# First layer of a hybrid S5/attention block: x loaded ahead of the S5 parameters, the norm and the first products in two halves of the channels, and the copies of u's rows on GpSimd

## The chip, the core and the metric

One core of one Trainium2 chip. The metric is the device time of one execution in microseconds, median of the runs; the profile is of one further execution.

## What is computed

Two layers over 256 tokens of 1024 channels in fp32. Each has a mixer (an S5 state-space mixer in layer 0, sparse attention in layer 1) and a PEER block; a conditioning vector c gives shift, scale and gate. The change touches layer 0's mixer alone:

```
mod = silu(c) @ ada_w[0] + ada_b[0];  sh1, sc1, g1, ... = split(mod, 6)
hm  = rmsnorm(x, norm1_g[0]) * (1 + sc1) + sh1
u   = hm @ w_in
dt  = exp(log_dt);  a_bar = exp(a*dt);  b_bar = (a_bar - 1)/a * B      # complex, 64 groups of 64 states
h_t = a_bar*h_{t-1} + b_bar u_t;   y_t = Re(C h_t) + d_skip*u_t
x   = x + g1 * (ya * sigmoid(yg)),  [ya, yg] = gelu(y) @ w_glu
```

## The kernel before

x lies transposed, channels on partitions, as eight chunks of 128 x 256 (`K.xT`, KC = 8). A weight comes from HBM in units of 512 KB (`load_unit`, L129, on SyncE's queue) into a ring of six `raw` buffers. Large products run as three fp32r products (`mm3`, L188 to L190): ScalarE rounds a unit to `w_hi` (L139), VectorE takes the rest as `w_lo` (L181); the activations are split the same way into `h_hi` (L303) and `h_lo` (L304).

The modulation comes in blocks of 512 values. `ada_block` makes four units' products into a row (L201) which ScalarE copies (L204); `ada_turn` turns it into a column per 128 channels (L213) and VectorE adds the bias (L216). Of shift 1 and scale 1, blocks 0 and 2 are the first four chunks' and blocks 1 and 3 the others'.

In the norm, squares (L249, ScalarE) are summed over channels by PE (L260); `rms_scale` makes a diagonal of reciprocal roots (L273 to L277), which one product spreads over the partitions (L279). `Norm` then multiplies by norm weight and scale (`scaled`, L297) and adds the shift (`shifted`).

`s5_params` (L339 to L424) computes a_bar, its powers and the turn angles with some 45 small VectorE instructions and ScalarE functions. `Tables.first(qt)` makes angles (L471 to L479), the B table (L452 on GpSimd, L454 and L455 on VectorE, placed by ScalarE in L462) and transposes it (L496, L497); `second(qt)` makes the C table the same way and T (L508 to L524). `s5_mix` runs the eight chunks of u: `copies` writes u with four time steps beside each other into `ust`, sixteen pieces of 32 x 64 per chunk (L580, ScalarE from PSUM), and u itself (L581); `states` multiplies by the windows (L589) and scans (L594 to L609, on VectorE but for L606 on GpSimd); `outputs` adds T u and C h (L618, L623), gelu and split. `after(i)` interleaves states of chunk i - 1, outputs of chunk i - 2, one table and one modulation block with chunk i's products. Then the w_glu products.

In `s5_layer` the order of PE and ScalarE is that of the source (`manual_schedule`); VectorE, GpSimd and SyncE are ordered by a scheduler. In `s5_mix` all engines are. Each engine and queue runs in its order.

Of the kernel before, what the change touches and what calls it, by code (L numbers as in the profile page):

```python
# [8 lines left out]
F32 = mybir.dt.float32  # L9
# [183 lines left out]
def ada_block(K, layer, n):  # L193

    nc = K.nc
    ps = bank(K)
    for k2 in range(KC // 2):
        w = load_unit(K, K.aps["ada_w"][n, k2]).rearrange("p (k n) -> p k n", k=2)
        for i in range(2):
            k = 2 * k2 + i  # L200
            nc.tensor.matmul(ps[32 * (k % 4):32 * (k % 4) + 32], K.cact[:, k, :], w[:, i, :],  # L201
                             start=(k < 4), stop=(k >= 4), skip_group_check=True)
    row = K.xp.tile([P, 512], F32, name="ada_row", bufs=1)
    nc.scalar.activation(row, ps, AF.Copy)  # L204
    return lambda: ada_turn(K, layer, n, row)

# [61 lines left out]

def rms_scale(K):

    nc = K.nc
# [6 lines left out]
    rs = bank(K)[:, :S]  # L278
    nc.tensor.matmul(rs, K.ones, diag.rearrange("p t n -> p (t n)"), start=True, stop=True)  # L279
    return rs  # L280


class Norm:


    def __init__(self, K, g, layer, part, rs, bufs=4):
        self.K, self.part, self.rs, self.bufs = K, part, rs, bufs
        self.mod = K.mod[layer]
        self.sc = K.xp.tile([P, KC], F32, name="nsc")
        K.nc.vector.scalar_tensor_tensor(self.sc, self.mod[:, part + 8:part + 16], 1.0, g, op0=OP.add, op1=OP.mult)  # L290
        self.hi = K.hpool.tile([P, KC, S], F32R, name="h_hi")
        self.lo = K.hpool.tile([P, KC, S], F32R, name="h_lo")
        self.t = K.xp.tile([P, KC, S], F32, name="nt")

    def scaled(self, k):
        K = self.K
# [42 lines left out]
def s5_params(K, pp, prm):  # L339
# [11 lines left out]
    with tc.tile_pool(name="s5q", bufs=1, reuse_waits="tile") as pr:  # L351
# [73 lines left out]
class Tables:  # L425
# [37 lines left out]

    def first(self, qt):

        K, pp = self.K, self.pp
# [20 lines left out]
        self.place(lambda r, g: self.b[r, :, :, :, g], m)  # L487
        for k in range(2 * qt, 2 * qt + 2):
# [39 lines left out]
def s5_layer(K):  # L528
    tc, nc = K.tc, K.nc
    with tc.tile_pool(name="s5p", bufs=1, reuse_waits="tile") as pp:  # L530
        prm = pp.tile([P, S5_W], F32, name="prm")
        nc.sync.dma_start(prm, K.aps["s5p"])
        nc.sync.dma_start(K.xT, K.aps["xT"])
        tab = Tables(K, pp)
        with tc.manual_schedule(engines={mybir.EngineType.PE, mybir.EngineType.Activation}):
            s5_params(K, pp, prm)
            sq_all(K)
            ada_block(K, 0, 2)()
            ada_block(K, 0, 3)()
# [9 lines left out]
            ada_block(K, 0, 1)()
            with tc.high_priority(offset=2 * PRIO):  # L550
                for k in range(4):
                    norm.shifted(k)
            with tc.high_priority(offset=2 * PRIO):
                for k in range(4, KC):
                    norm.shifted(k)
            for k in range(4):
                pair.add(k)
            for k in range(4, KC):
                pair.add(k)
            tab.second(0)  # L560
        s5_mix(K, pp, h, tab, pair.ps)


def s5_mix(K, tp, h, tab, first):
# [858 lines left out]
```

## Time and profile before

| | us |
|---|---|
| median of 3 runs (lowest, highest) | 2085.86 (2085.52, 2088.15) |
| the profiled execution, and its span | 2086.9, 2085.1 |
| busy in the span: PE, DVE, ACT, POOL | 2020.8, 1582.5, 1170.4, 111.1 |

PE is TensorE, DVE VectorE, ACT ScalarE, POOL GpSimd, SP SyncE's queue; PEld is PE's weight loads. Busy time is a sum over the whole span, which has stages with different limits, so the rows below are taken by stage. An instruction's row gives its start from the span's start, its length, and in brackets how long its engine sat idle before it and who ended that. A matmul's end is modelled.

### The profile page before, as it was taken

What the parts mean: (1) busy time and instruction counts of PE and PEld (TensorE: products, weight loads), DVE (VectorE), ACT (ScalarE), POOL (GpSimd) and SP (SyncE); (2) the same over time, 40 slices, a digit from 0 to 9 for tenths busy, and PEclk for the clock granted to TensorE, in tenths of its full rate; (3) what the DMA queues carried; (4) which work ended last, traced back from release to release, by engine and by line L of the source; (5) the groups of instructions that cost most, each with busy time, mean ns of one, the idle gap of its engine ahead of it and who ended that gap; (6) DMA issues with size and microseconds to landing.
All of it is one profiled execution on the core that took longest, in us unless ns stands there. A gap on an engine that the chain in (4) does not pass through costs nothing. (4 is left out here: it accounts for less than half of the span.)

```text
span 2085.1 us, 39099 instructions
## 1 busy us (share of the span) xinstructions
PE 2020.8 (97%) x14344; PEld 1838.7 (88%) x14344; DVE 1582.5 (76%) x3593; ACT 1170.4 (56%) x2412; POOL 111.1 (5%) x103
## 2 busy tenths in 40 slices
PE   6899999999999999999999999999999999999998
PEld 3679999899999988888888789999999998888887
DVE  5776899878887777777775869998788865555665
ACT  4985555554445555555555755555454455555554
POOL 3210001300000000000010000022000000000000
PEclk9999999999999999999999999999999999999998
DMA  6445555544445888888863045555444456666663
GB/s 258 181 173 163 162 174 171 161 151 135 142 142 179 260 277 267 272 270 268 276 225 112 22 142 163 172 166 166 135 142 142 142 174 187 195 193 194 192 195 97
DMA packets 102688, 377.17 MB, mean 181 GB/s; under 512 B 11488, under 2 KB 11872, under 8 KB 101472
## 3 DMA queue, kind: packets, MB, share of 16 engines
q1 hardware_dynamic: 101520, 371.42, 56.0%
q0 software_dynamic: 544, 2.61, 0.4%
q8 instruction: 112, 1.84, 0.4%
q14 instruction: 80, 0.66, 0.1%
q10 hardware_dynamic: 432, 0.65, 0.1%
HBM read 373.07 MB, written 1.05 MB: 179 GB/s over the span
## 5 line engine op out<-in xcount | busy, mean ns | idle before, releaser
L139 ACT ACTIVATE w_hi<-raw 128x512 fp32r<-128x512 f32 x1194 | 746.7, 628 | 734.3 <-PE bank L189 433.6
L181 DVE TENSOR_TENSOR w_lo<-raw,w_hi 128x512 fp32r<-128x512 f32 x1194 | 816.9, 706 | 135.0 <-ACT w_hi L139 133.1
L188 PE MATMUL bank<-h_hi,w_hi 128*128 128x256 f32 x2504 | 716.6, 289 | 7.2 <-ACT h_hi L303 3.3
L190 PE MATMUL bank<-h_hi,w_lo 128*128 128x256 f32 x2504 | 708.2, 285 | 11.0 <-DVE w_lo L181 11.0
L189 PE MATMUL bank<-h_lo,w_hi 128*128 128x256 f32 x2504 | 708.9, 284 | 0.7 <-DVE h_lo L304 0.7
L188 PEld LDWEIGHTS bank<-h_hi,w_hi 128*128 128x128 f32 x2504 | 484.6, 194 | 15.8 <-ACT h_hi L303 4.9
L190 PEld LDWEIGHTS bank<-h_hi,w_lo 128*128 128x128 f32 x2504 | 480.1, 193 | 14.7 <-DVE w_lo L181 14.4
L189 PEld LDWEIGHTS bank<-h_lo,w_hi 128*128 128x128 f32 x2504 | 482.7, 193 | 2.7 <-DVE h_lo L304 1.6
L804 PE MATMUL bank<-w_lo,a_hi 128*128 128x512 f32 x1024 | 398.8, 389 | 0.2 <-DVE w_lo L181 0.2
L804 PE MATMUL bank<-w_hi,a_lo 128*128 128x512 f32 x1024 | 398.5, 389 | 0.0
L804 PE MATMUL bank<-w_hi,a_hi 128*128 128x512 f32 x1024 | 281.0, 389 | 0.0
L181 DVE TENSOR_TENSOR a_lo<-B,a_hi 128x256 fp32r<-128x256 f32 x256 | 108.9, 425 | 198.0 <-ACT a_hi L139 198.0
L804 PEld LDWEIGHTS bank<-w_hi,a_lo 128*128 128x128 f32 x1024 | 192.3, 188 | 40.0
L804 PEld LDWEIGHTS bank<-w_lo,a_hi 128*128 128x128 f32 x1024 | 192.3, 188 | 39.7 <-DVE w_lo L181 0.7
L804 PEld LDWEIGHTS bank<-w_hi,a_hi 128*128 128x128 f32 x1024 | 191.5, 188 | 38.5
L775 PE MATMUL bank<-ohl,oij 128*128 128x128 f16 x1024 | 129.2, 307 | 0.0
L139 ACT ACTIVATE a_hi<-B 128x256 fp32r<-128x256 f32 x256 | 106.8, 418 | 27.2 <-PE bank L804 14.4
L778 DVE SCALAR_TENSOR_TENSOR B<-bank,B 128x216 f32<-128x216 f32 (+31 forms) x128 | 62.6, 489 | 71.8 <-PE bank L775 71.1
L775 PEld LDWEIGHTS <-oij 128*128 128x128 f16 x1024 | 101.5, 128 | 4.2
L770 DVE TENSOR_TENSOR ohl<-oij,slotT 128x1024 f16<-128x1024 f16 x128 | 90.7, 710 | 0.1
L767 DVE TENSOR_TENSOR oij<-iota,slotT 128x1024 f16<-128x1024 f16 x128 | 87.1, 682 | 0.0
L938 POOL TENSOR_TENSOR B<-B 128x512 f32<-128x512 f32 x32 | 55.2, 1732 | 331.5 <-DVE B L936 331.5
(262 smaller groups left out, 1771.7 us busy)
## 6 DMA issues: line engine op xcount, KB each, us to landing
raw<-peer_u SPq DMA_DIRECT2D x256, 512.0 KB, 3.6
raw<-peer_v SPq DMA_DIRECT2D x256, 512.0 KB, 4.3
raw<-ada_t SPq DMA_DIRECT2D x56, 512.0 KB, 4.5
raw<-ada_w SPq DMA_DIRECT2D x40, 512.0 KB, 5.2
raw<-w_q SPq DMA_DIRECT2D x32, 512.0 KB, 3.5
raw<-w_glu SPq DMA_DIRECT2D x16, 512.0 KB, 4.1
raw<-w_in SPq DMA_DIRECT2D x8, 512.0 KB, 6.4
w<-w_cmp SPq DMA_DIRECT2D x4, 1024.0 KB, 9.8
```

What stands on the lines that cost most here:

```text
L139: nc.scalar.activation(hi, raw, AF.Copy)
L181: K.nc.vector.tensor_tensor(lo, raw, hi.bitcast(F32), op=OP.subtract)
L188: nc.tensor.matmul(out, wh, xh, start=start, stop=False)
L189: nc.tensor.matmul(out, wh, xl, start=False, stop=False)
L190: nc.tensor.matmul(out, wl, xh, start=False, stop=stop)
L767: V.tensor_tensor(oij.rearrange("p a n j t -> p (a n) j t"), tab[:, None].to_broadcast(full), si, op=OP.is_equal)
L770: V.tensor_tensor(ohl, oj, slotT[:, 1, 2 * q:2 * q + 2, :, None, :].to_broadcast([P, 2, 2, P, 2]), op=OP.mult)
L775: nc.tensor.matmul(pv[:, :, t], oij[:, t // 2, 0, :, t % 2], ohl[:, t // 2, n, :, t % 2], start=(n == 0), stop=(n == 1), skip_group_check= ...
L778: V.scalar_tensor_tensor(B[:, :jd, ts], pv[:, :jd], 1.0 / GS, B[:, :jd, ts], op0=OP.mult, op1=OP.mult)
L804: nc.tensor.matmul(acc[t][dh], a[al][:, ts], w[wl], start=(j == 0 and al + wl == 0), stop=(j == NJ - 1 and al == 1))
L938: nc.gpsimd.tensor_mul(eq[:, c, hs], eq[:, c, hs], idf[:, t, hs, c, None, :].to_broadcast(shape))
```

## The change

x comes in two halves as SyncE's first loads; of s5p the small part comes first on ScalarE's queue, the rest (B and C) behind the first two w_in units. The squares are summed by VectorE (L568) before PE sums over partitions. The parameters stop ahead of the sines (`yield`), so that the norm's scale goes between. Blocks 2 and 0 come first, then norm, shift and products of chunks 0 to 3, then angles and B table, blocks 3 and 1, and the same for chunks 4 to 7. The order of all five engines in `s5_layer` is now that of the source. In `s5_mix` ScalarE copies u once, and GpSimd copies the sixteen pieces from it. `rms_scale` is cut in two, `Norm.scales` may be called by halves, `first` is cut into `angles` and `inputs`; elsewhere these give the same instructions, and behind the first w_glu products the engines' order is the same as before.

```diff
-    row = K.xp.tile([P, 512], F32, name="ada_row", bufs=1)
+    row = K.xp.tile([P, 512], F32, name="ada_row", bufs=2)
...
-        nc.sync.dma_start(prm, K.aps["s5p"])
-        nc.sync.dma_start(K.xT, K.aps["xT"])
-        tab = Tables(K, pp)
-        with tc.manual_schedule(engines={mybir.EngineType.PE, mybir.EngineType.Activation}):
-            s5_params(K, pp, prm)
-            sq_all(K)
-            ada_block(K, 0, 2)()
-            ada_block(K, 0, 3)()
-            rs = rms_scale(K)
-            tab.first(0)
-            norm = Norm(K, small(K, "n1g")[:, 0:8], 0, 0, rs, KC)
...
+        nc.scalar.dma_start(prm[:, small_], K.aps["s5p"][:, small_])
+        with tc.manual_schedule(engines={E.PE, E.Activation, E.DVE, E.SP, E.Pool}):
+            for i in range(2):
+                ks = slice(4 * i, 4 * i + 4)
+                nc.sync.dma_start(K.xT[:, ks], K.aps["xT"][:, ks])
+            tab = Tables(K, pp)
+            K.sq = bank(K)
+            for k in range(KC):
+                sq = K.xp.tile([P, S], F32, name="sq" if k else "sqt", bufs=3 if k else 1)
+                nc.scalar.activation(sq, K.xT[:, k], AF.Square)
+                if k:
+                    nc.vector.tensor_add(total, total, sq)
...
+            par = s5_params(K, pp, prm)
+            next(par)
+            scale = ada_block(K, 0, 2)
...
+            diag = rms_diag(K)
+            next(par, None)
+            shift = ada_block(K, 0, 0)
+            scale()
+            rs = rms_row(K, diag)
+            shift()
+            norm = Norm(K, small(K, "n1g")[:, 0:8], 0, 0, rs, 4, late=True)
+            norm.scales(0, 4)
+            for k in range(4):
+                norm.scaled(k)
             pair = Pair(K, [K.aps["w_in"][0], K.aps["w_in"][1]], h)
+            nc.sync.dma_start(prm[:, large], K.aps["s5p"][:, large])
...
             for k in range(4):
                 pair.add(k)
+            nc.gpsimd.tensor_scalar(K.cmat[:, 1], K.cmat[:, 1], -1.0, None, op0=OP.mult)
+            tab.angles(0)
+            scale = ada_block(K, 0, 3)
+            tab.inputs(0)
+            shift = ada_block(K, 0, 1)
+            scale()
+            norm.scales(4, KC)
...
-        pv = ps.rearrange("p (c s) -> p s c", s=L)
+        nc.scalar.activation(u, ps.rearrange("p (c s) -> p s c", s=L), AF.Copy)
         for q in range(4):
             for t in range(L):
-                src, dst = pv[32 * q:32 * q + 32, t], ust[32 * t:32 * t + 32, q]
-                nc.scalar.activation(dst, src, AF.Copy)
-        nc.scalar.activation(u, pv, AF.Copy)
+                nc.gpsimd.tensor_copy(ust[32 * t:32 * t + 32, q], u[32 * q:32 * q + 32, t])
```

PE ahead of the first w_in products, before (L201 are units of modulation blocks: here block 0 into `bank_346`; L213 a turn, L496 the B table's transposes):

```order
L213 MATMUL bank_271<-ones_73,ada_row_269 128x1 x4
L279 MATMUL bank_283<-rs_281,ones_73 128x256
L496 MATMUL bank_308<-cst_69,bpad_92 128x128 x4
L496 MATMUL bank_314<-cst_69,bpad_92 128x128 x4
L496 MATMUL bank_321<-cst_69,bpad_92 128x128 x4
L496 MATMUL bank_327<-cst_69,bpad_92 128x128 x4
L201 MATMUL bank_346<-raw_347,cact_81 32x512 x2
L201 MATMUL bank_346<-raw_351,cact_81 32x512 x2
L201 MATMUL bank_346<-raw_355,cact_81 32x512 x2
L201 MATMUL bank_346<-raw_359,cact_81 32x512 x2
L213 MATMUL bank_365<-ones_73,ada_row_363 128x1 x4
```

And now (block 0 goes into `bank_245`; L575 sums the squares, L276 spreads the diagonal):

```order
L575 MATMUL bank_111<-ones_73,sqt_112 128x1 x2
L201 MATMUL bank_245<-raw_246,cact_81 32x512 x2
L201 MATMUL bank_245<-raw_250,cact_81 32x512 x2
L201 MATMUL bank_245<-raw_254,cact_81 32x512 x2
L201 MATMUL bank_245<-raw_258,cact_81 32x512 x2
L213 MATMUL bank_264<-ones_73,ada_row_173 128x1 x4
L276 MATMUL bank_270<-rs_181,ones_73 128x256
L213 MATMUL bank_272<-ones_73,ada_row_262 128x1 x4
L188 MATMUL bank_307<-h_hi_279,w_hi_289 128x256
```

The transposes no longer stand between the norm's row and block 0, and blocks 3 and 1 stand behind the first half of the products.

VectorE from the last parameter instruction on, before (L454, L455 the B table; L471 to L474 angles; L290 the scale):

```order
L375 TENSOR_SCALAR s5keep<-s5keep 128x64
L454 TENSOR_TENSOR cm_298<-s5keep,prm 128x512 x2
L273 TENSOR_SCALAR ms<-bank 128x2
L455 TENSOR_TENSOR cm_298<-cm_298,cm_299 128x1024
L216 TENSOR_TENSOR mod_75<-bank,sm 128x4
L275 RECIPROCAL ms<-ms 128x2
L277 TENSOR_TENSOR rs<-cst,ms 128x256
```

And now (L469, L470 are that B table, L490 to L493 angles, L312 the norm's products, L319 `h_lo`):

```order
L390 TENSOR_SCALAR s5keep<-s5keep 128x64
L216 TENSOR_TENSOR mod_75<-bank,sm 128x4 x2
L307 SCALAR_TENSOR_TENSOR nsc<-mod_75,sm 128x4
L312 SCALAR_TENSOR_TENSOR nt<-xT,nsc,bank 128x256 x4
L181 TENSOR_TENSOR w_lo<-raw,w_hi 128x512 x4
L319 SCALAR_TENSOR_TENSOR h_lo<-nt,mod_75,h_hi 128x256 x4
L490 TENSOR_TENSOR ang<-cst,s5turn 128x512
L492 TENSOR_SCALAR angn<-ang 128x512
L493 TENSOR_TENSOR ang<-ang,angn 128x512
L469 TENSOR_TENSOR cm_356<-s5keep,prm 128x512 x2
L470 TENSOR_TENSOR cm_356<-cm_356,cm_357 128x1024
```

The norm's first half now stands behind the parameters, which it does not read, and ahead of the B table.

GpSimd in the first chunks, before (L452 its half of a table, L606 its product of the scan):

```order
L452 TENSOR_TENSOR cm1_782<-s5keep_110,prm_89 128x512 x2
L452 TENSOR_TENSOR cm1_976<-s5keep_110,prm_89 128x512 x2
L606 TENSOR_TENSOR rB_572<-rS_573,sinT_290 128x256
L452 TENSOR_TENSOR cm1_1157<-s5keep_110,prm_89 128x512 x2
L481 MEMSET r4_597 128x8
L606 TENSOR_TENSOR rB_723<-rS_724,sinT_290 128x256
```

And now (L467 and L652 are these two, L627 the copies):

```order
L627 COPY ust_520<-u_540 32x64 x16
L467 TENSOR_TENSOR cm1_778<-s5keep_135,prm_89 128x512 x2
L627 COPY ust_520<-u_656 32x64 x16
L467 TENSOR_TENSOR cm1_972<-s5keep_135,prm_89 128x512 x2
L652 TENSOR_TENSOR rB_568<-rS_569,sinT_348 128x256
L627 COPY ust_520<-u_839 32x64 x16
L467 TENSOR_TENSOR cm1_1153<-s5keep_135,prm_89 128x512 x2
L500 MEMSET r4_593 128x8
L652 TENSOR_TENSOR rB_719<-rS_720,sinT_348 128x256
```

Sixteen copies a chunk stand between the tables and the scan's products; each burst reads u from SBUF and waits until PE has read the burst before it.

## Rows read from the trace of the kernel before

**Rows 1.** Busy time by stage. Columns: stretch in us, its length, busy us (and instructions) of the five engines' rows, granted PE clock as a share of full speed, DMA share, GB/s. PE's first sum of squares starts at 10.70, the first w_in products at 51.26, the first output table's products (L518) at 57.22, chunk 2's products at 74.00, the first w_glu products at 152.81.

```profile
0.00:10.70 10.70, 0.00 (x0) 0.00 (x1) 3.68 (x25) 5.11 (x10) 10.11 (x15) 1.00 0.83 320
10.70:51.26 40.56, 30.80 (x146) 18.39 (x147) 24.63 (x61) 20.28 (x37) 7.55 (x7) 0.96 0.64 239
57.22:74.00 16.78, 11.62 (x105) 8.44 (x104) 10.58 (x19) 15.74 (x53) 5.09 (x5) 0.80 0.41 148
74.00:152.81 78.81, 71.04 (x937) 60.63 (x937) 62.60 (x124) 69.77 (x191) 14.61 (x15) 0.94 0.50 184
152.81:203.00 50.19, 49.05 (x524) 48.52 (x522) 33.97 (x63) 27.94 (x54) 4.98 (x6) 1.00 0.52 158
```

**Rows 2.** PE's timeline: start and length in us, line, operation, and the idle time before it with its releaser.

```profile
45.30 4.29 PE L201 MATMUL bank<-raw,cact 128*32 128x512 f32 x16
50.35 1.05 PE L213 MATMUL bank<-ones,ada_row 128*128 128x1 f32 x8 [0.76 <-ACT ada_row L204]
...
65.67 3.67 PE L496 MATMUL bank<-cst,bpad 128*128 128x128 f32 x16 [3.35 <-ACT bpad L462]
...
91.79 1.97 PE L496 MATMUL bank<-cst,bpad 128*128 128x128 f32 x16
```

**Rows 3.** The waits of PE from 57.22 to 157.9: who waited for whom, us in total, times, longest.

```profile
PE bank L496 <- ACT bpad L462: 3.3, 1, 3.3
PE bank L213 <- ACT ada_row L204: 2.7, 2, 2.0
PE bank L589 <- ACT ust L580: 2.2, 5, 0.6
PE bank L188 <- ACT u L581: 2.2, 1, 2.2
PE bank L188 <- ACT w_hi L139: 1.7, 1, 1.7
```

**Rows 4.** Busy time in three short stretches, columns as in rows 1.

```profile
4.00:6.00 2.00, 0.00 (x0) 0.00 (x0) 0.01 (x1) 0.01 (x1) 2.00 (x4) 1.00 1.01 416
...
34.00:40.00 6.00, 4.41 (x24) 3.57 (x28) 5.89 (x12) 4.70 (x9) 0.23 (x1) 1.00 0.01 3
46.00:50.00 4.00, 3.59 (x12) 0.38 (x8) 1.38 (x3) 0.64 (x2) 0.00 (x0) 0.57 0.87 290
```

**Rows 5.** ACT's groups of instructions from 57.22 to 152.81: busy us and mean ns of one, then the idle time before them.

```profile
L580 ACT ACTIVATE ust<-bank 32x64 f32<-32x64 f32 x128 | 27.4, 214 | 2.1
...
L522 ACT ACTIVATE T<-bank 32x128 f32<-32x128 f32 x32 | 8.5, 266 | 0.4
L497 ACT ACTIVATE win<-bank 128x512 f32<-128x512 f32 x12 | 6.6, 593 | 0.1
L462 ACT ACTIVATE bpad<-cm 64x1024 f32<-64x1024 f32 x6 | 6.3, 1056 | 0.1
...
L626 ACT ACT_TABLE_LOAD x3 | 3.8, 1283 | 0.1
```

**Rows 6.** DMA issues up to 60 us: KB each and us from issue to landing. This one is issued at 1.18.

```profile
cst<-consts ACTq DMA_DIRECT2D x1, 128.0 KB, 7.8
```

**Rows 7.** DVE's timeline, columns as in rows 2.

```profile
7.92 0.19 DVE L375 TENSOR_SCALAR sp<-sp 128x32 f32<-128x32 f32 x1
...
11.93 0.43 DVE L473 TENSOR_SCALAR angn<-ang 128x512 f32<-128x512 f32 x1
...
12.56 0.68 DVE L474 TENSOR_TENSOR ang<-ang,angn 128x512 f32<-128x512 f32 x1
...
16.58 0.20 DVE L375 TENSOR_SCALAR s5keep<-s5keep 128x64 f32<-128x64 f32 x1
...
33.34 3.22 DVE L297 SCALAR_TENSOR_TENSOR nt<-xT,nsc,bank 128x256 f32<-128x256 f32 x8
...
37.07 1.29 DVE L454 TENSOR_TENSOR cm<-s5keep,prm 128x512 f32<-128x512 f32 x2
38.46 1.23 DVE L455 TENSOR_TENSOR cm<-cm,cm 128x1024 f32<-128x1024 f32 x1
...
40.40 1.15 DVE L473 TENSOR_SCALAR angn<-ang 128x512 f32<-128x512 f32 x1
41.58 1.47 DVE L474 TENSOR_TENSOR ang<-ang,angn 128x512 f32<-128x512 f32 x1
...
45.49 1.89 DVE L181 TENSOR_TENSOR w_lo<-raw,w_hi 128x512 fp32r<-128x512 f32 x3
50.72 1.68 DVE L304 SCALAR_TENSOR_TENSOR h_lo<-nt,mod,h_hi 128x256 fp32r<-128x256 f32 x4 [3.34 <-ACT h_hi L303]
```

**Rows 8.** POOL's timeline, columns as in rows 2. In the first row DVE is idle.

```profile
21.21 2.17 POOL L452 TENSOR_TENSOR cm<-s5keep,prm 128x512 f32<-128x512 f32 x2 [1.96 <-DVE cm L455]
39.77 2.74 POOL L452 TENSOR_TENSOR cm<-s5keep,prm 128x512 f32<-128x512 f32 x2 [16.39 <-DVE cm L455]
...
72.28 0.75 POOL L606 TENSOR_TENSOR rB<-rS,sinT 128x256 f32<-128x256 f32 x1 [1.28 <-DVE rS L602]
```

**Rows 9.** POOL's groups of instructions in the whole span, columns as in rows 5.

```profile
L606 POOL TENSOR_TENSOR rB<-rS,sinT 128x256 f32<-128x256 f32 x8 | 7.8, 975 | 31.3 <-DVE rS L602 24.3 <-ACT u L581 7.0
...
L1015 POOL CAST maskb<-nsac 128x128 bf16<-128x128 f32 x1 | 0.3, 290 | 7.8 <-DMA nsac<-nsa_c 7.8
L1056 POOL MEMSET kp<- 64x64 f32 x2 | 0.2, 146 | 0.1
```

More of the change, by code (lines that the diff above doesn't have):

```diff
@@ L269, in rms_scale, with rms_row, rms_diag @@
 def rms_scale(K):
+    return rms_row(K, rms_diag(K))
+def rms_row(K, diag):
+    rs = bank(K)[:, :S]
+    K.nc.tensor.matmul(rs, K.ones, diag.rearrange("p t n -> p (t n)"), start=True, stop=True)
+    return rs
+def rms_diag(K):
     nc = K.nc
@@ L277, in rms_scale, with __init__, scales @@
     nc.vector.tensor_mul(diag, K.ident[:, None].to_broadcast([P, 2, P]), ms[:, :, None].to_broadcast([P, 2, P]))
-    rs = bank(K)[:, :S]
-    nc.tensor.matmul(rs, K.ones, diag.rearrange("p t n -> p (t n)"), start=True, stop=True)
-    return rs
+    return diag
 class Norm:
-    def __init__(self, K, g, layer, part, rs, bufs=4):
+    def __init__(self, K, g, layer, part, rs, bufs=4, late=False):
         self.K, self.part, self.rs, self.bufs = K, part, rs, bufs
-        self.mod = K.mod[layer]
+        self.mod, self.g = K.mod[layer], g
         self.sc = K.xp.tile([P, KC], F32, name="nsc")
-        K.nc.vector.scalar_tensor_tensor(self.sc, self.mod[:, part + 8:part + 16], 1.0, g, op0=OP.add, op1=OP.mult)
+        if not late:
+            self.scales(0, KC)
         self.hi = K.hpool.tile([P, KC, S], F32R, name="h_hi")
         self.lo = K.hpool.tile([P, KC, S], F32R, name="h_lo")
-        self.t = K.xp.tile([P, KC, S], F32, name="nt")
+        self.t = K.xp.tile([P, bufs, S], F32, name="nt")
+    def scales(self, k0, k1):
+        p = self.part + 8
+        self.K.nc.vector.scalar_tensor_tensor(self.sc[:, k0:k1], self.mod[:, p + k0:p + k1], 1.0, self.g[:, k0:k1],
+                                              op0=OP.add, op1=OP.mult)
     def scaled(self, k):
@@ L379, in s5_params @@
         nc.scalar.activation(dt, ldt, AF.Exp)
-        nc.gpsimd.tensor_scalar(K.cmat[:, 1], K.cmat[:, 1], -1.0, None, op0=OP.mult)
         x = mul(are, dt)
@@ L389, in s5_params @@
         ts(thr, PI_LO, -PI_LO, OP.min, OP.max, o=thr)
+        yield
         sn, sh = t(), t()
@@ L464, in first, with angles @@
     def first(self, qt):
+        self.angles(qt)
+        self.inputs(qt)
+    def angles(self, qt):
         K, pp = self.K, self.pp
@@ L487, in first, with inputs @@
         self.place(lambda r, g: self.b[r, :, :, :, g], m)
+    def inputs(self, qt):
+        K, pp = self.K, self.pp
+        nc = K.nc
         for k in range(2 * qt, 2 * qt + 2):
@@ L531, in s5_layer @@
         prm = pp.tile([P, S5_W], F32, name="prm")
-        nc.sync.dma_start(prm, K.aps["s5p"])
-        nc.sync.dma_start(K.xT, K.aps["xT"])
-        tab = Tables(K, pp)
-        with tc.manual_schedule(engines={mybir.EngineType.PE, mybir.EngineType.Activation}):
-            s5_params(K, pp, prm)
-            sq_all(K)
-            ada_block(K, 0, 2)()
-            ada_block(K, 0, 3)()
-            rs = rms_scale(K)
-            tab.first(0)
-            norm = Norm(K, small(K, "n1g")[:, 0:8], 0, 0, rs, KC)
-            with tc.high_priority(offset=2 * PRIO):
-                for k in range(KC):
-                    norm.scaled(k)
+        small_, large = slice(0, 3 * NP2), slice(3 * NP2, S5_W)
@@ new lines, in s5_layer @@
+        nc.scalar.dma_start(prm[:, small_], K.aps["s5p"][:, small_])
+        E = mybir.EngineType
+        with tc.manual_schedule(engines={E.PE, E.Activation, E.DVE, E.SP, E.Pool}):
[9 more added lines that the diff above has]
+                    nc.vector.tensor_add(total, total, sq)
+                else:
+                    total = sq
+            par = s5_params(K, pp, prm)
+            next(par)
+            scale = ada_block(K, 0, 2)
+            for t in range(2):
+                nc.tensor.matmul(K.sq[:, t:t + 1], total[:, t * P:(t + 1) * P], K.ones[:, 0:1],
+                                 start=(t == 0), stop=True, skip_group_check=True)
+            diag = rms_diag(K)
[5 more added lines that the diff above has]
+            norm = Norm(K, small(K, "n1g")[:, 0:8], 0, 0, rs, 4, late=True)
@@ L546, in s5_layer @@
             h = (norm.hi, norm.lo)
-            ada_block(K, 0, 0)()
+            norm.scales(0, 4)
+            for k in range(4):
+                norm.scaled(k)
             pair = Pair(K, [K.aps["w_in"][0], K.aps["w_in"][1]], h)
[L549 to L555, printed above, removed]
+            nc.sync.dma_start(prm[:, large], K.aps["s5p"][:, large])
@@ L556, in s5_layer @@
+            for k in range(4):
+                norm.shifted(k)
             for k in range(4):
                 pair.add(k)
+            nc.gpsimd.tensor_scalar(K.cmat[:, 1], K.cmat[:, 1], -1.0, None, op0=OP.mult)
[5 more added lines that the diff above has]
+            norm.scales(4, KC)
+            for k in range(4, KC):
+                norm.scaled(k)
+            shift()
+            for k in range(4, KC):
+                norm.shifted(k)
```

## The prediction

> **What bounds the kernel now.** I read the profile in this order: the stages of the first 203 us, what PE waited for in them, then the instructions that end those waits. Behind the first w_glu products (152.81) the order stays as it is, and PE is 98% busy up to 203 [rows 1], so time won before that point is won for the whole kernel, and the question is when each stage ends.
>
> The stages are five [rows 1]: squares and parameters to 10.70; modulation, norm and tables to 51.26; the first pair of products to 57.22; the first outputs to 74.00, where chunk 2's products start; and six chunk periods to 152.81, where the w_glu products start. In the second stage DMA is the resource, and it lies idle: 416 GB/s when it runs, 3 GB/s between 34 and 40 us [rows 4], because the raw tiles of block 0 are read only behind the transposes, which wait for the first B table. In the last two stages ACT is the fullest: 15.74 of 16.78 us and 69.77 of 78.81 us [rows 1]; of this the copies into ust take 27.4 us [rows 5]. The waits of PE there, 12.1 us in the five largest, nearly all end on ACT [rows 3]. So PE (71.04 busy) is close behind, and DVE (62.60) is third.
>
> **The front, up to the first outputs (57.22 now).** DMA: 320 GB/s over 10.70 us [rows 1] is 3.42 MB. In the new order that is the small tables (0.26 MB), x (1.05) and block 2 (2.10), so block 2 is there at 10.7. At 416 GB/s [rows 4] block 0 is there at 15.8, the two w_in tiles at 18.3, the rest of s5p at 20.8, block 3 at 25.9.
>
> The norm ends later than block 0, because of DVE's written order. Its cast of the constants stands ahead of the sum of squares, and consts land 7.8 us after their issue [rows 6], at 9.0. Seven additions at 0.40 (as each of the eight in the norm's 3.22 us [rows 7]): 11.8. The first part of the parameters: a table load of 1.28 [rows 5] and some eight small instructions, 14. Mean square, the root's table load, reciprocal and diagonal: 16. Then the rest of the parameters, which now stands ahead of the modulation: from 7.92 to 16.78 today, 8.9 us, of which about 2 are angle steps that go elsewhere and about 1 belongs to the first part [rows 7]; 6 us, so 22. PE's turns of blocks 2 and 0 (1.05 each at full clock [rows 2]) and the row product are over by about 19, so they are not what ends last. From there: modulation 0.4, four nt 1.6, four w_lo 2.5 (1.89 for three), four h_lo 1.7 [rows 7]: 28.2. GpSimd's first tables run under this and take about 1 us from DVE (below). The first half of the products ends near 30.
>
> Behind it on DVE stand the angles (1.6) and the B table (1.29 and 1.23 [rows 7]): 33.3; placing it costs ACT 2.11 [rows 5]: 35.4. The sixteen transposes take 2.0 to 3.7 us, block 1 takes 1.9 to 4.3, by the clock [rows 2]. Its last two tiles are loaded into buffers that block 3 frees at 30 to 31, and land by about 34: hidden. PE's clock was granted 0.57 of full speed while it waited in a like place [rows 4], so I take neither end: 40.5 (39.3 to 43.3). Turn, second half of nt, shift and products follow in 6.5 us: 47. DVE has the last h_lo at 45.5; then the first C table, 2.5 and 2.1 to place it: 50.1. That table is ready early today, and is the one thing that the written order makes later. So the first outputs start 7 us earlier than at 57.22 (bounds 4 and 9).
>
> **From there to chunk 2 (16.78 us now).** 32 copies leave ACT. What is left on its path there: two copies of u, T, the C part, the B table's placing, a row, four windows and w_hi, about 10 us: T eight times 0.27, the placing 2.11, four windows of 0.59 [rows 5], and some 3 for the rest. PE's order (transposes, a block, states ahead of chunk 2) adds 2 to 3. I take 12.3: 4.5 us less (3.5 to 5).
>
> **Six chunk periods (78.81 us now, 13.1 each).** ACT loses 96 copies of 214 ns, 20.5 us [rows 5], and falls to 49. GpSimd gets 112 (chunk 0's sixteen lie ahead). The trace has no such copy on GpSimd. Its nearest rows: 64 elements written only, 0.146 us; 128 read and written, 0.290 [rows 9]. I take 0.15, since its length is the former's, and keep 0.29; below, a cost of nothing would need DVE never to be in the way.
>
> It is in the way: in the angle steps at 40.40 and 41.58 DVE took 1.15 and 1.47 us for what takes 0.43 and 0.68 alone, while GpSimd took 2.74 for two products that take 2.17 alone [rows 7, 8]. Together 2.1 us were lost to an overlap of about 2.7. So most of what GpSimd reads while DVE works is added to one of the two. DVE is busy 79% of this stage, some 85% of that with both inputs in SBUF, so two thirds of the copies' time falls on it: 112 x 0.15 x 0.67 = 11 us. DVE also gets chunk 0's states, which run before 74.00 today, 4.7 us. DVE: 62.6 + 11 + 4.7 = 78.3. That is the next bound, where ACT's was, and the stage gains next to nothing: 1 us. With no such loss it would be PE's 71.04 less its slow stretches: up to 11 us gained. With 0.29 us a copy it is 10 us worse. The Trainium skill (SBUF — State Buffer, "Who interferes with whom") says that "a DVE instruction with two SBUF inputs contends with a GpSimd instruction that reads SBUF", and that one with a PSUM input does not. The two angle steps agree as far as they go. By it every copy would be exclusive with those instructions for its whole length, which puts the stage about 5 us above my sum.
>
> Moved x, s5p and SP's queue: the six raw buffers are freed in a new order, but a chunk needs 2.6 MB, 6.3 us at 416 GB/s, of 13. The negation of C on GpSimd now waits for the rest of s5p (20.8); some 1.5 us (512 elements, between the rows 9), and behind it stand only tables that DVE reads at 32. u now comes first on ACT and frees its bank 3 us earlier, worth nothing by itself.
>
> **Sum.** 7 + 4.5 + 1 = 12.5 us. The profiled execution took 2086.9; that gives 2074.4. The median of the three runs is 1.0 lower, 2085.86, so I say **2073.4**. About 0.2% (4.2 us) is what a measurement of this kernel can tell from no change.
>
> **Rivals.** *PE becomes the bound.* If the copies slip in between DVE's instructions, the last stage gains 11 instead of 1: 2063.4. For it: PE's waits all ended on ACT [rows 3], and DVE has 21% of idle time. Against: the stretched angle steps. 0.17.
>
> *The front gives its gain back.* The half clock in transposes and block 1, and the late C table, leave 4 us there, and DVE's load takes the gain of the next stage: 2081 to 2085. For it: 0.57 granted at 46 to 50 [rows 4]. 0.06.
>
> *Copies at the upper bound*, 0.29: 10 us back, 2083.5. 0.07.
>
> *GpSimd becomes the bound, and the kernel slower.* A copy from one group of 32 partitions to another may cost far more than rows on equal partitions show, and each may wait for a DVE instruction ahead of it. GpSimd works 14.61 / 6 = 2.4 us per chunk now [rows 1]; sixteen copies of p make 16 p + 2.4. Above p = 0.67 that exceeds 13.1, at 0.79 it has eaten 11.5 us, and above 0.83 the kernel is measurably slower; at 1 us a copy, 2106. PE then waits for ust in its order, as it did for ACT. For it: the product of 256 elements takes 0.975 us on average beside DVE, 0.75 at best [rows 8, 9]. Against: the short rows, 0.146 and 0.290. 0.08.
>
> **Numbers.** Forecast 0.62, its own range 2067 to 2080 (front 4 to 9, next stage 3.5 to 5, last stage from 5 gained to 3 lost). Faster: forecast and PE-bound, 0.79. Same: the two that give the gain back, 0.13. Slower: 0.08. The range from 2062 to 2084 leaves out the slower case, part of the PE-bound one, and little else.
>
> **What would show it.** In the new profile: first products of the first half at about 25 to 30 us, DMA without a gap until 25; first outputs at 50; chunk 2 at 62; w_glu products at 140. COPY on GpSimd at 0.15 to 0.3 us; DVE over 90% busy in the chunk periods, its scans and tables longer than now; PE's waits there ended by DVE or GpSimd instead of ACT. I am wrong if DVE stays below 85% and PE has no waits (PE-bound), if COPY lasts over 0.6 us, or if the first half of the products starts after 35.

## The result, and the profile after

The changed kernel takes **2070.81 us** (median of six, 2070.11 to 2072.01) against 2087.01 for the kernel before on the same chip: a ratio of 0.9921, 95% interval [0.9909, 0.9933]. The forecast was 2073.4, faster, in a range of 2062 to 2084. The profiled execution took 2071.75 us with a span of 2069.9, against 2086.9 and 2085.1.

So the total and its sign came as forecast. The terms did not: the front and the stage behind it gave less, and the six chunk periods gave nine times what I had put down. That the total came out near is luck, since errors of opposite sign made up for each other.

First the stages, with the columns of [rows 1]. The first half of the products starts at 26.64, block 3 is over by 36.6, the second half starts at 45.54, the first output table's products at 51.99, chunk 2's products at 66.30, the w_glu products at 136.04.

```profile
8.28:26.64 18.36, 11.80 (x55) 4.09 (x55) 14.61 (x62) 10.37 (x20) 4.74 (x7) 0.92 1.01 407
26.64:34.50 7.86, 5.00 (x24) 4.71 (x24) 7.69 (x16) 3.30 (x8) 0.00 (x0) 0.54 0.40 137
34.50:45.50 11.00, 8.15 (x67) 4.65 (x65) 8.09 (x14) 8.89 (x16) 2.74 (x2) 0.94 0.77 281
45.50:51.99 6.49, 5.67 (x25) 5.27 (x25) 4.18 (x8) 4.09 (x8) 2.18 (x2) 0.58 0.44 174
51.99:66.30 14.31, 12.38 (x105) 8.14 (x105) 8.49 (x15) 11.92 (x23) 10.30 (x26) 0.88 0.54 184
66.30:136.04 69.74, 65.39 (x926) 56.48 (x925) 62.66 (x120) 47.52 (x92) 57.40 (x119) 1.00 0.56 205
136.04:186.00 49.96, 49.38 (x525) 48.70 (x524) 34.91 (x68) 26.71 (x51) 6.99 (x12) 1.00 0.48 149
```

| | before | after | gain | forecast |
|---|---|---|---|---|
| first outputs | 57.22 | 51.99 | 5.2 | 7 |
| from there to chunk 2 | 16.78 | 14.31 | 2.5 | 4.5 |
| six chunk periods | 78.81 | 69.74 | 9.1 | 1 |

Up to 136.04 that makes 16.8 us. A mark further on counts better, since a part of the last chunks' work lies on either side of 136: the row product of the second norm stands at 205.1 before and at 190.5 after, 14.5 us earlier. From it to the end of the span it is 1880.0 and 1879.4 us, the same.

In the chunk periods DVE is 62.66 us busy, as before (62.60 in [rows 1]), although GpSimd went from 14.61 to 57.40. But it has four instructions fewer there, some 2.2 us of work. What became of single instructions (line, shape, count, busy us and mean ns of one, idle time before), on DVE before:

```profile
L181 DVE TENSOR_TENSOR w_lo<-raw,w_hi 128x512 fp32r<-128x512 f32 x16 | 12.0, 770 | 7.4 <-ACT w_hi L139 7.4
L602 DVE TENSOR_TENSOR_SCAN rS<-r,rA 128x256 f32<-128x256 f32 x14 | 9.9, 739 | 0.0
L454 DVE TENSOR_TENSOR cm<-s5keep,prm 128x512 f32<-128x512 f32 x8 | 5.2, 687 | 3.9 <-ACT bpad L462 3.3 <-ACT wo L462 0.5
L455 DVE TENSOR_TENSOR cm<-cm,cm 128x1024 f32<-128x1024 f32 x4 | 4.9, 1222 | 0.1
```

And after:

```profile
L181 DVE TENSOR_TENSOR w_lo<-raw,w_hi 128x512 fp32r<-128x512 f32 x14 | 10.3, 745 | 1.8 <-ACT w_hi L139 1.8
L648 DVE TENSOR_TENSOR_SCAN rS<-r,rA 128x256 f32<-128x256 f32 x14 | 9.2, 693 | 0.0
L469 DVE TENSOR_TENSOR cm<-s5keep,prm 128x512 f32<-128x512 f32 x8 | 6.7, 875 | 0.0
L470 DVE TENSOR_TENSOR cm<-cm,cm 128x1024 f32<-128x1024 f32 x4 | 6.0, 1490 | 1.0 <-POOL cm L467 1.0
L654 DVE TENSOR_TENSOR rH<-rH,rB 128x256 f32<-128x256 f32 x6 | 2.5, 421 | 3.4 <-POOL rB L652 3.4
```

And on GpSimd:

```profile
L627 POOL COPY ust<-u 32x64 f32<-32x64 f32 x102 | 42.2, 413 | 9.0 <-ACT u L624 4.7
L467 POOL TENSOR_TENSOR cm<-s5keep,prm 128x512 f32<-128x512 f32 x8 | 10.3, 1306 | 3.1 <-DVE cm L470 2.8
L652 POOL TENSOR_TENSOR rB<-rS,sinT 128x256 f32<-128x256 f32 x6 | 5.3, 876 | 0.2
```

A copy takes 0.41 us, not 0.15. But the VectorE instructions that met the copies hardly grew: w_lo takes 0.745 (0.770 before), the scan 0.693 (0.739 before), while L469 and L470, some of which meet GpSimd's products, went from 0.687 to 0.875 and from 1.222 to 1.490. These means mix instructions that ran beside different things. Sorted in the two traces by what GpSimd did meanwhile, w_lo takes 0.68 us beside nothing and 0.70 beside copies; all 91 instructions beside copies alone took 1.0 us longer together than their like beside nothing, and the 15 that met a product 5.9 us (before: 23, and 4.3 us).

PE's waits from the first outputs to the w_glu products, which all but 0.8 us ended on ACT before (the largest are in [rows 3]), now are these (who waited for whom, us, times, longest):

```profile
PE bank L635 <- POOL ust L627: 3.0, 5, 0.8
PE bank L669 <- DVE rH L654: 2.8, 2, 1.6
PE bank L541 <- POOL cm L467: 0.8, 1, 0.8
PE bank L519 <- ACT bpad L477: 0.4, 1, 0.4
```

Together 7 us. PE is now the fullest engine, 65.39 of 69.74 us in the chunk periods.

### The profile page after: what moved, and what is told of

It reads as the page before. It is cut to its first block, busy times and chain, and to the rows that moved or that the text cites. A ratio compares the mean times of both kernels' runs of the same rounds, so it can differ in the third digit from the quotient of the medians.

```text
span 2069.9 us, 39056 instructions
## 1 busy us (share of the span) xinstructions
PE 2011.1 (97%) x14316; PEld 1828.9 (88%) x14316; DVE 1590.8 (77%) x3601; ACT 1143.3 (55%) x2283; POOL 149.8 (7%) x231
## 5 line engine op out<-in xcount | busy, mean ns | idle before, releaser
L190 PEld LDWEIGHTS bank<-h_hi,w_lo 128*128 128x128 f32 x2504 | 481.0, 193 | 14.3 <-DVE w_lo L181 14.0
L984 POOL TENSOR_TENSOR B<-B 128x512 f32<-128x512 f32 x32 | 44.2, 1382 | 340.8 <-DVE B L982 340.8
```

The source lines that it names most:

```text
L190: nc.tensor.matmul(out, wl, xh, start=False, stop=stop)
L984: nc.gpsimd.tensor_mul(eq[:, c, hs], eq[:, c, hs], idf[:, t, hs, c, None, :].to_broadcast(shape))
```

## The experiments

Times of one kernel lie up to 9 us apart (nine of the kernel before, on one chip: 2086.16 to 2095.48), so a median alone doesn't settle 2 or 3 us. Beside the ratios I use two marks of each profile: the length from the first outputs to the first w_glu products, and the row product of norm 2. Each ratio is to runs of the kernel before on the same chip. The front has its own scatter: in the runs whose code is the same up to there, first outputs come at 50.8 to 52.3.

| | median | ratio to before, interval | first outputs | to w_glu | norm 2's row |
|---|---|---|---|---|---|
| before | 2087.01 | | 57.22 | 95.59 | 205.1 |
| the change | 2070.81 | 0.9921 [0.9909, 0.9933] | 51.99 | 84.05 | 190.5 |
| 1 front alone | 2083.62 | 0.9974 [0.9964, 0.9984] | 51.12 | 100.21 | 203.8 |
| 2 copies alone | 2079.55 | 0.9956 [0.9940, 0.9971] | 55.79 | 86.52 | 196.8 |
| 3 copies twice | 2115.14 | 1.0123 [1.0102, 1.0144] | 52.33 | 125.46 | 232.6 |
| 4 half on ACT | 2074.58 | 0.9932 [0.9912, 0.9953] | 50.84 | 87.98 | 190.1 |
| 6 inputs late | 2073.54 | 0.9926 [0.9900, 0.9952] | 54.17 | 83.92 | 192.6 |
| 7 rB on DVE | 2077.97 | 0.9949 [0.9929, 0.9969] | 52.10 | 88.03 | 194.4 |
| 8 products on DVE | 2072.16 | 0.9919 [0.9893, 0.9945] | 55.51 | 81.27 | 191.1 |
| 9 ust twice | 2073.74 | 0.9925 [0.9911, 0.9938] | 51.45 | 85.81 | 191.6 |
| 10 cm1 twice | 2074.03 | 0.9929 [0.9915, 0.9944] | 53.24 | 81.92 | 189.7 |
| 11 is 8 and 9 | 2069.25 | 0.9903 [0.9887, 0.9919] | 53.18 | 80.11 | 187.5 |
| 12 is 11, front as changed | 2071.53 | 0.9912 [0.9893, 0.9931] | 51.90 | 82.32 | 188.4 |

**1. The front alone.** The changed kernel, with the copies of the kernel before:

```diff
-        nc.scalar.activation(u, ps.rearrange("p (c s) -> p s c", s=L), AF.Copy)
-                nc.gpsimd.tensor_copy(ust[32 * t:32 * t + 32, q], u[32 * q:32 * q + 32, t])
+                nc.scalar.activation(dst, src, AF.Copy)
+        nc.scalar.activation(u, pv, AF.Copy)
```

> The changed kernel with the sixteen copies back on ScalarE from PSUM, as before. Theory A (two separate gains: the front's new order, and ScalarE's relief in the chunk periods): the front keeps its 5 us, first outputs at 52, the six chunk periods take some 79 us again, total 2082 (2080 to 2084). Theory B (most of the gain is the written order of all engines in the front and what it brings into the chunks): 2073 to 2076, since the copies give back what they take.

**2. The copies alone**, the reverse of this edit, in the kernel before.

> The kernel before with the sixteen copies moved to GpSimd and nothing else. Theory A (ScalarE was the bound from the first outputs on; a copy takes 0.40 us on GpSimd but costs VectorE almost nothing): first outputs stay at 57, chunk periods 70 us, total 2074 to 2077. Theory B (the prediction's: the copies take VectorE's time, some 11 us, and VectorE becomes the bound): 2085 to 2088.

Both theories A came near, though 2 is 2.6 us above its range. By the ratios, 0.26% and 0.44% add up to the 0.79% of the change within their intervals. The profiles tell how unlike the two are: the front's first outputs come 6.1 us earlier, and of that 1.5 are left at the w_glu products. Here is the front alone, from its first outputs to chunk 2's first products and from there to the w_glu products:

```profile
51.12:69.11 17.99, 13.61 (x104) 8.95 (x104) 13.03 (x21) 16.99 (x54) 5.91 (x5) 0.74 0.36 122
69.11:151.33 82.22, 71.24 (x941) 60.91 (x937) 63.38 (x125) 68.78 (x190) 15.21 (x16) 0.94 0.48 179
```

ACT is 16.99 of 17.99 us busy, and behind that a rounding of w_in waited 5.44 us for its tile (2.47 before, at 79.58):

```profile
76.45 1.15 ACT L139 ACTIVATE w_hi<-raw 128x512 fp32r<-128x512 f32 x2 [5.44 <-DMA raw<-w_in]
```

That tile stands on SP's queue behind four modulation tiles, whose buffers PE frees, and PE waited 4.2 us for the B table's placing on ACT. So in this profile, where ACT sets the pace, an earlier front is mostly lost. The times leave more of it: 0.26% is 5.4 us, with an interval of 3.3 to 7.5. Which of the two is right isn't settled. With the copies away, the stage takes 84 to 87 us with either front.

**3. Each copy made twice**, the second time into a tile that nothing reads:

```diff
                 nc.gpsimd.tensor_copy(ust[32 * t:32 * t + 32, q], u[32 * q:32 * q + 32, t])
+                nc.gpsimd.tensor_copy(spare[32 * t:32 * t + 32, q], u[32 * q:32 * q + 32, t])
```

> The changed kernel with every one of the sixteen copies made twice, the second time into a tile that nothing reads. Theory A: GpSimd needs 32 x 0.41 + 2.7 = 15.8 us per chunk where a period takes 11.6, so GpSimd becomes the bound and six periods and the stage ahead cost some 28 us more: 2096 to 2102; VectorE's instructions keep their lengths within 5%, products of GpSimd apart. Theory B (copies take VectorE's time, 0.1 us each): VectorE's instructions with two inputs in SBUF grow by a fifth or more (w_lo from 0.745 to over 0.85).

The direction and the place are those of theory A, the size is not: 44 us above the change where 28 were expected. VectorE's lengths did stay (w_lo 0.716, the scan 0.690). GpSimd's two lines of copies, and PE's waits:

```profile
L628 POOL COPY ust<-u 32x64 f32<-32x64 f32 x128 | 44.8, 350 | 12.8 <-PE bank L637 6.6 <-ACT u L625 0.4
L629 POOL COPY spare<-u 32x64 f32<-32x64 f32 x128 | 40.3, 315 | 6.9 <-ACT u L625 2.0
```

```profile
PE bank L637 <- POOL ust L628: 10.0, 4, 5.6
PE bank L541 <- ACT wo L477: 7.6, 3, 3.2
PE bank L519 <- ACT bpad L477: 7.6, 3, 4.9
```

Each copy is cheaper than 0.41. GpSimd is busy 102.5 of the stage's 125.5 us, and of the idle 20 us ahead of its copies some 11 are the gaps from one copy to the next (0.04 us each). That makes 113 us, about what my price gives (84 and 28). The rest is a circle: a burst waits until PE has read the one before (6.6 us), and PE waits for the burst (10.0 us). On top of that PE runs the same instructions in 100.1 instead of 77.8 us, at a granted clock of 0.78 of full speed instead of 0.98 (the levels are 1.2 and 2.4 GHz): behind its waits PE runs slowly, too. My price was throughput alone, and such a chain costs more.

**4. Eight copies on ACT, eight on GpSimd** (`if q < 2:` ACT from PSUM).

> The changed kernel with eight of the sixteen copies on ScalarE from PSUM and eight on GpSimd. Theory A (GpSimd is now as near to the bound as PE: its bursts end waits of PE, 3.0 us, and delay rB, 3.4 us of VectorE's waits): GpSimd falls from 57 to 36 us of the chunk periods, both waits go, total 2066 to 2069. Theory C (PE alone is the bound now, with 65.4 of 69.7 us): 2070 to 2072, no change.

Nearer to theory C, as far as 4 times from 2070.2 to 2075.7 can tell (their median is above its range, too): GpSimd fell from 67.7 to 40.6 us from the first outputs on, and norm 2's row came at 190.1 instead of 190.5.

**5. The contention by itself.** A piece of work ahead of the mixer: 128 x 512 products on VectorE, both inputs in SBUF, six alone and sixteen beside GpSimd, and four kinds of work on GpSimd, alone and beside them. Only its trace is of use, since the work is added to the kernel:

```diff
+            for tag, fn, alone, n in (("x", cross, 8, 24), ("e", same, 8, 24), ("w", wide, 4, 10), ("p", prod, 4, 10)):
+                fn(go, last, alone)
+                dve(da, go, 6)
+                fn(gb, da, n)
+                dve(db, b, 16)
```

> The changed kernel with a piece of measuring work put ahead of the mixer, which reads and writes tiles of its own: on VectorE products of 128 x 512 with both inputs in SBUF (0.68 us alone in the chunk periods), six by themselves and then sixteen while GpSimd works; on GpSimd, each kind first by itself and then beside them: copies of 32 x 64 between different groups of 32 partitions, the same within one group, copies of 128 x 512, products of 128 x 256. Theory A (copies give way to VectorE, products don't): beside copies of 32 x 64 VectorE's product takes 0.68 to 0.75 and the copy grows from 0.40 to 0.50; beside products VectorE's takes 1.1 or more on average. Theory B (every instruction of GpSimd that reads SBUF holds VectorE off for its whole length): VectorE's sixteen products take longer by the whole of the copies' time, to 1.2 us on average, beside copies as beside products. The copy within one group tells whether 0.40 is the price of changing partitions (then it takes 0.15 to 0.2) or of any copy (0.35 to 0.40).

GpSimd's timeline (start, length of the row, count): each kind alone, then beside VectorE. Beside the first row VectorE only writes (memsets).

```profile
3.23 2.14 POOL L565 COPY mgox<-ma 32x64 f32<-32x64 f32 x8 [2.18 <-DVE mgox L585]
...
28.00 2.14 POOL L571 COPY mgoe<-mdlx 32x64 f32<-32x64 f32 x8 [0.79 <-DVE mdlx L597]
34.55 13.85 POOL L571 COPY mgbe<-mdae 32x64 f32<-32x64 f32 x24 [4.42 <-DVE mdae L560]
49.19 2.64 POOL L576 COPY mgow<-mdle 128x512 f32<-128x512 f32 x4 [0.79 <-DVE mdle L597]
56.25 10.15 POOL L576 COPY mgbw<-mdaw 128x512 f32<-128x512 f32 x10 [4.42 <-DVE mdaw L560]
71.44 3.13 POOL L580 TENSOR_TENSOR mgop<-mdlw,msrc 128x256 f32<-128x256 f32 x4 [5.05 <-DVE mdlw L597]
79.01 11.27 POOL L580 TENSOR_TENSOR mgbp<-mdap,msrc 128x256 f32<-128x256 f32 x10 [4.44 <-DVE mdap L560]
```

VectorE's, in the same stretches: six alone, then sixteen beside GpSimd.

```profile
30.17 4.32 DVE L560 TENSOR_TENSOR mdae<-mgoe,mbb 128x512 f32<-128x512 f32 x6 [2.23 <-POOL mgoe L571]
34.41 11.58 DVE L560 TENSOR_TENSOR mdbe<-mbb 128x512 f32<-128x512 f32 x16
...
56.10 14.46 DVE L560 TENSOR_TENSOR mdbw<-mbb 128x512 f32<-128x512 f32 x16
...
78.85 15.61 DVE L560 TENSOR_TENSOR mdbp<-mbb 128x512 f32<-128x512 f32 x16
```

A product takes 0.72 us alone (4.32 / 6). Beside copies of 32 x 64 it takes 0.72 (11.58 / 16): nothing lost. Beside wide copies it loses 2.9 us over ten of them, 0.29 each, of the 0.66 that one takes alone; beside products 4.1 us, 0.41 each of 0.78. GpSimd gets in once per VectorE instruction: beside VectorE's sixteen products, which end at 45.99, sixteen copies start, one every 0.73 us, and the eight left follow every 0.29, nearly as they do alone. So a pair lasts 0.73, 1.01 and 1.13 us: what exceeds about 0.36 us of GpSimd's instruction is added to VectorE, and a copy of 0.27 is below that (an estimate from these rows, for these products). The copy between different groups of partitions costs what one within a group does, 2.14 for eight.

Theory A, with two corrections. A copy alone is 0.23 us long and the next starts 0.27 us behind it; in the changed kernel these are 0.41 and 0.45. And that growth is its wait for VectorE: from 51.99 to 136.04 the 36 copies that met no VectorE instruction, or only such as read PSUM, are 0.23 us long, as alone, and the other 88 on average 0.47.

**6. The transposes later**: `tab.inputs(0)` behind `tab.second(0)`.

> The changed kernel with the first table's sixteen transposes and four copies (inputs) behind the second half of the products and the C table, instead of between modulation blocks 3 and 1. Theory A (the second half waits in PE's order behind the transposes, which wait for the placing of the B table): block 1 follows block 3 at 36.6, the second half starts at 42 instead of 45.5, first outputs at 49 instead of 52; chunk 2 at 64 to 66; total 2068 to 2071. Theory B (half clock and the raw tiles of block 1 set that pace, or the time is lost again ahead of chunk 2, where windows are then late): first outputs at 51 to 52, total 2071 to 2074.

The time is theory B's (2073.54), the reason neither's: the second half starts later, at 47.70. Without the transposes PE stands before block 1 and waits for its last two raw tiles:

```profile
40.07 1.61 PE L201 MATMUL bank<-raw,cact 128*32 128x512 f32 x4 [2.77 <-DMA raw<-ada_w]
42.04 1.92 PE L201 MATMUL bank<-raw,cact 128*32 128x512 f32 x4 [0.37 <-DMA raw<-ada_w]
```

So in the changed kernel, too, the transposes fill a wait that is there anyway. The further 2 us are those tiles: the last came later than the 41.7 at which block 1 ends in the changed kernel. From 39 to 42 us DMA moved 272 GB/s here and 422 there; why is left open.

**7. rB on VectorE**, and **8. all of GpSimd's products on VectorE**:

```diff
-        nc.gpsimd.tensor_mul(B[:, 0], sc[:, 1], sink)
+        nc.vector.tensor_mul(B[:, 0], sc[:, 1], sink)
```

```diff
-            nc.gpsimd.tensor_mul(m1[:, c], *times(1 - c, signs[c]))
+            nc.vector.tensor_mul(m1[:, c], *times(1 - c, signs[c]))
```

> The changed kernel with the scan's one product of GpSimd (rB, 0.73 to 1.17 us) on VectorE. Theory A (GpSimd's products and not its copies slow VectorE, and VectorE's waits for rB, 3.4 us, with PE's for rH, 2.8 us, come from them): VectorE gets 8 x 0.41 = 3.3 us of work and loses the 3.4 us of waits and some 3 us of slow neighbours; first w_glu products 2 to 3 us earlier, total 2068 to 2070. Theory B (VectorE, 62.7 of 69.7 us busy, is the bound): 3 us later, 2073 to 2075.

> The changed kernel with all products of GpSimd (rB, and two of each table's four, 2.2 to 2.7 us for two) on VectorE; GpSimd keeps the copies. Theory A (GpSimd's products cost VectorE about as much as they take themselves): VectorE gets 3.3 us and seven times 1.3 us of tables and loses 3.4 us of waits and some 7 us of slowed instructions, its w_lo goes to 0.70 and its C and B sums from 1.40 to 1.25 us: about even, 2069 to 2073. Theory B (GpSimd's products are free help): VectorE's 62.7 us become 71 and with it the stage: 2078 to 2081.

Experiment 7 went against theory A. The loss is near theory B's, 4 us at norm 2's row, but did not come through VectorE, which is busy 73.1 of 88.0 us. GpSimd's own waits show it (from 50 to 138 us; 11.5 of the 15.8 lie ahead of the first outputs, as in the changed kernel):

```profile
POOL cm L467 <- DVE cm L470: 15.8, 2, 11.5
POOL ust L627 <- PE bank L635: 13.2, 4, 6.8
```

In its new order GpSimd took up a table at 99.22 whose tile VectorE still had to read, waited 4.3 us, and made it beside the scans in 4.57 us where 2.7 is usual; the copies queued behind it, and PE waited 5.9 us for ust in all, 4.3 of it for these copies. Experiment 8 came out as theory A says: VectorE's L470 falls back to 1.220 us (1.402 from the first outputs on in the changed kernel), w_lo to 0.694 (0.740), and VectorE's busy time rises by 2.3 us only, for 6.7 us of table products and 3.0 of rB. The stage is 2.8 us shorter; the front pays, with first outputs at 55.51 (53.18 in experiment 11, whose code up to there is the same).

**9. Two buffers of ust, 10. two of cm1, 11. edits 8 and 9 together, 12. as 11 with the first two tables as in the change.**

```diff
+        ust = sts[k] = tp.tile([P, 4, 64], F32, name="ust", bufs=2)
```

```diff
-        m1 = self.pp.tile([P, 2, QP, L, 16], F32, name="cm1", bufs=1)
+        m1 = self.pp.tile([P, 2, QP, L, 16], F32, name="cm1", bufs=2)
```

```diff
+        eng = self.K.nc.vector if hs.start else self.K.nc.gpsimd
```

> The changed kernel with ust in two buffers in turn, so that a burst of copies doesn't wait for PE's reading of the one before (2.6 us of GpSimd's waits from the first outputs on; PE's own waits for ust 3.0 us). Theory A (PE is within some 6 us of its own work from the first outputs to the w_glu products, and what is left are waits for GpSimd's bursts): PE's waits for ust fall to 1 us or less, total 1 to 3 us less than the changed kernel's 2070.8: 2068 to 2070. Theory B (bursts are late because they stand behind tables and scan products in GpSimd's order, not for want of a buffer): 2070 to 2072.

> The changed kernel with two buffers for GpSimd's half of a table (cm1), so that its products don't wait for VectorE's sum of the table before (2.8 us before the burst at 103 us); the squares' ring goes from three buffers to two to make room. Theory A (that wait holds up the copies behind it, and PE with them): GpSimd runs ahead with tables, bursts come earlier, total 2068 to 2070. Theory B (tables that run ahead are GpSimd's products beside VectorE at another place, and copies wait behind them): 2070 to 2074.

> Two buffers of ust, and all products of GpSimd on VectorE: GpSimd has the copies alone. Theory A (with nothing ahead of the copies and a buffer free, no engine waits for GpSimd, and VectorE's 78 of 88 us leave room): PE's waits for ust go, total 2068 to 2071. Theory B (VectorE is then the bound: each of its delays reaches PE through rH or the tables): 2071 to 2074, as with the products alone (2072.2).

> Two buffers of ust, GpSimd's products from the second pair of chunks on and all rB on VectorE; the first pair's two tables keep their halves on GpSimd, since VectorE is the chain of the front. Theory A (with all products on VectorE the first C table came 1.3 us later, first outputs at 53.2 instead of 52.0, while the chunk periods lost PE's waits): first outputs at 51 to 52, PE's waits for ust and rH under 2 us up to the w_glu products, norm 2's row at 186 to 187.5 instead of 190.5, total 2066 to 2069. Theory B (the chunk periods start from whatever time VectorE and PE allow, so that the 1.2 us are not passed on): 2069 to 2070, as with all products on VectorE (2069.25).

A buffer alone gained nothing that can be seen (9: PE's waits for ust fell only to 2.0, those for rH rose to 5.2; 10: norm 2's row 0.8 us earlier, the times not lower). In 11 hardly a wait is left, and PE works 78.57 of 80.11 us:

```profile
53.18:133.29 80.11, 78.57 (x1029) 66.06 (x1029) 73.46 (x151) 58.29 (x113) 50.03 (x122) 0.94 0.58 211
```

It is the fastest by its median, 0.9903 of before. Its interval overlaps the change's, and 12, which should have been better still, scattered from 2066.3 to 2076.7. Its first outputs came at 51.9 as theory A has it, but PE still waited 4.0 us for ust, and norm 2's row, at 188.4, missed the theory's 187.5. So that either beats the changed kernel isn't shown.

## Why the prediction was right

**ACT was the bound, and the copies leaving it are the gain: right.** Experiment 2 has this part alone, and PE's waits went from ACT to GpSimd and VectorE.

**The copies on GpSimd: mis-sized twice.** I took 0.15 us and kept 0.29; from start to start 0.27 is the price alone, near the CAST of [rows 9] and far from the MEMSET I took, and 0.45 in place. Even so, 16 x 0.45 and 2.6 us of other work make 10 us of a period of 11.6, below the bound, so the rival in which GpSimd decides stayed away. Experiment 3 shows it when the copies are doubled.

**VectorE as the next bound: wrong, and this is the failed step.** I put 11 us of the copies' time and 4.7 us of chunk 0's states on VectorE, and got 78.3 busy. It measured 62.66, and the loss beside copies, 11 us in my sum, is 1.0. The first term was read off two angle steps beside GpSimd's products [rows 7, 8]; that reading is right for products (0.41 of 0.78 lost in experiment 5) and is next to nothing for a short copy. I carried a loss per us of GpSimd's time over to another kind of instruction. The second term forgot the other end: the scans are fourteen in both stretches, since chunk 7's states fell behind the first w_glu products. The Trainium skill (SBUF — State Buffer, "SBUF: two separate sides") says that whichever starts first, a VectorE instruction with two SBUF inputs or a GpSimd one that reads SBUF, holds the shared port pair for the whole instruction, and the other blocks. Turn by turn agrees with experiment 5; the cost for VectorE doesn't: 0, 0.29 and 0.41 us beside instructions of 0.27, 0.66 and 0.78.

So the periods went nearly as in the rival that has PE as the bound (11 gained; 9.1 measured), and what hid this in the total is that the two terms ahead fell short by 3.8. That is luck: with those two right and the periods as measured my sum would have been 20.6 us and the forecast 2065.3, outside my own range of 2067 to 2080.

**The front: 1.8 us short, in one term for the most part.** The diagonal was over at 16.5 (I had said 16). The rest of the parameters then took VectorE until 24.2, 7.75 us instead of 6:

```profile
16.48 0.17 DVE L390 TENSOR_SCALAR sp<-sp 128x32 f32<-128x32 f32 x1
...
18.78 0.18 DVE L390 TENSOR_SCALAR sp<-sp 128x32 f32<-128x32 f32 x1
19.00 0.19 DVE L375 TENSOR_TENSOR sp<-sp,sp 128x32 f32<-128x32 f32 x1
...
24.23 0.22 DVE L216 TENSOR_TENSOR mod<-bank,sm 128x4 f32<-128x4 f32 x2
```

There is no other work between these small instructions, and one of 128 x 32 that reads what the one right before it wrote starts 0.22 us behind it, the others 0.09 to 0.12. What stands behind is shifted by that: the C table is placed at 51.9 instead of 50.1. (Block 1 gave 1 us back, ending 4 us behind the B table's placing instead of 5; half a us each was lost at the diagonal and behind block 1.) The half clock was in other places than I had looked for: not in the transposes and block 1 (0.94 granted), but in both halves of the products (0.54 and 0.58), each of which starts behind a wait of PE. It was so in [rows 4] too: PE was not waiting at 0.57, as I wrote, but busy 3.59 of 4.00 us; its wait, of 3.21 us, had ended at 44.32. The rows of the changed kernel:

```profile
26.64 0.58 PE L188 MATMUL bank<-h_hi,w_hi 128*128 128x256 f32 x1 [6.10 <-ACT h_hi L318]
30.07 0.58 PE L189 MATMUL bank<-h_lo,w_hi 128*128 128x256 f32 x1 [2.86 <-DVE h_lo L319]
...
39.65 2.15 PE L201 MATMUL bank<-raw,cact 128*32 128x512 f32 x16
...
45.54 0.58 PE L188 MATMUL bank<-h_hi,w_hi 128*128 128x256 f32 x1 [1.32 <-ACT h_hi L318]
```

And "hidden" was too much said of block 1's last tiles. Block 3, which frees their buffers, ran from 34.7 to 36.6 and not at 30 to 31, and experiment 6 shows them landing at 40 to 42: only the transposes ahead cover that.

**To chunk 2: 2.0 us short.** I reckoned with ACT and PE alone. GpSimd's first burst ends at 58.8, a table of 2.5 us stands behind it, and the second burst waits 2.6 us for PE; GpSimd is 10.3 of 14.3 us busy. PE waited 1.6 us for ust and ran the transposes behind that in 3.48 us, where 1.94 was enough at 37.78. That these make the 2.0 is read from one trace and not tested.

**Front and copies may not simply add.** I summed them as if each were worth its own time. At norm 2's row of one profile each they make 1.3 and 8.3 us apart, and 14.5 together. In the times the sum and the whole can't be told apart (0.26% and 0.44% against 0.79%). So that the front alone loses most of its 6.1 us before the w_glu products is what one profile shows, and no more.

**A sign that didn't tell.** I had named "VectorE over 90% busy" as the mark of my theory. It is at 90%, but because the periods became shorter, with VectorE's busy time unchanged. The mark to name would have been the length of its instructions.

## What to carry to other kernels

When work moves to an engine that shares something with a fuller one, price the loss by the same kind of instruction, alone and beside the other, and not by the time that the engine is busy: short copies on GpSimd cost VectorE next to nothing here, its products about half their length. A gain ahead of a stage that another engine bounds can be lost there (one profile shows it, the times do not settle it), so look at a mark behind that stage before two gains are added. And a burst on an in-order engine pays for whatever is queued before it: one product moved away from GpSimd made the kernel slower, all of them and a second buffer did not.

## What was not expected of the hardware

- GpSimd's fp32 copy of 32 x 64 takes 0.27 us alone, whether or not it changes the group of partitions, and 0.73 beside back-to-back products of 0.72 on VectorE, which lose nothing; its 128 x 512 copy takes 0.66, only two and a half times as long for sixteen times the elements (0.27 and 0.66 are spacings).
- VectorE's cast of 128 x 256 took 1.93 us beside GpSimd's large memsets in the changed kernel (1.13, 1.39 and 1.48 in experiments 1, 8 and 11), and 0.28 without them in experiment 5. GpSimd's memset beside it, and the cast:

```profile
5.84 2.24 POOL L450 MEMSET wo<- 128x2560 f32 x1
6.76 1.93 DVE L62 CAST iota<-cst 128x256 f16<-128x256 f32 x1 [1.08 <-DMA cst<-consts]
```
